# Two feed-forward networks of a four-layer transformer whose up products all read the un-normalised residual, and a norm spread over one of them

## The chip, the cores and the metric

The kernel runs on one core of a Trainium2 chip. The metric is the device time of one execution in microseconds (us). The engines are TensorE (PE: matmuls, with PEld for its weight loads), VectorE (DVE), ScalarE (ACT), GpSimd (POOL) and SyncE (SP), which here issues the DMAs of the weights.

## The reference

Two blocks of two layers each work on 256 context tokens and 256 latent tokens of 1024 features. A layer is a mixer (attention with pooling and gating in layers 0 and 1, mLSTM in layer 2, sliding-window attention in layer 3) and then a feed-forward network (FFN) with a squared relu. Each reads a root-mean-square norm of the residual with a scale and a shift per feature that come from a conditioning vector:

```python
h = h + g1 * mix
h = h + g2 * sq_relu_mlp(modulate(rms_norm(h, norm2_g[l]), sh2, sc2), w_ff1[l], w_ff2[l])
# rms_norm(x, g): x * rsqrt(mean(x*x) + eps) * g;  modulate(h, shift, scale): h * (1 + scale) + shift
# sq_relu_mlp(h, w1, w2): square(relu(h @ w1)) @ w2;  w1 is 1024 x 4096, w2 4096 x 1024
...
return rms_norm(h, final_g)          # end of the first block, layers 0 and 1
```

The second block starts from the first one's latent output and from a context of its own, ctx_2. Layers 1 and 3 are the last of their blocks: their FFNs work on the latent tokens alone.

## The kernel before

Features lie on the 128 partitions in KT = 8 chunks, tokens on the free axis, so the residual `h` is 128 x 8 x 512, context first (L = 256). A product is made in fp32r pairs: `whi·xhi`, `whi·xlo` and `wlo·xhi`, three matmuls, called a triple here. A weight tile of 512 KB (128 x 1024) comes by DMA into a staging tile (`raw` or `Y`), ScalarE copies it to `whi` (L116), and VectorE, or GpSimd where `self.wlow` says so, subtracts to get `wlo` (L130). Three buffers each hold `whi` and `wlo`; results go round the PSUM banks `mm`, `mm`, `mx`.

An FFN (`mlp`) has 32 up tiles and 32 down tiles, in eight groups q of four: `up(0)`, then `up(q)` and `down(q - 1)` in turn, and `down(7)` last. After an up tile ScalarE applies the relu, VectorE squares (L643), ScalarE makes the high part and VectorE the low part (L648) of the hidden tile. After a down tile VectorE adds to `h` (`add_to_h`, shown as h<-mm or h<-mx).

A norm begins in `add_to_h`: `square` lets ScalarE square a chunk of `h` that was just written, and GpSimd add it to `sums` (L509) for chunks 1 to 6, while the last square stays alone. `variance` lets TensorE multiply both with the constant `mean` (rows T<-mean), VectorE add eps (L521) and GpSimd take the power -0.5 (L522). `rows` spreads the result over the partitions (T<-ident). `modulate` then makes the high and low part of the normed chunk k with two VectorE instructions and one of ScalarE.

The generators given as `pre` and `mid` are advanced after so many steps of a group of three interleaved tiles, the numbers in `PRE` and `MID`; `PLAIN` is for the plain start. This start is what layers 1 and 3 have: their first three up tiles don't wait for the norm. They multiply the scaled residual (`plain_xs`, in the `Y` tiles), plus two columns with the shift, hence 258 columns; `evac_plain` then multiplies the result with the factor R (L659) and hands the extra column to the relu as its bias. From tile 4 on the FFN reads the normed `xs`. While this goes on GpSimd makes the low parts of the weights.

The first block's closing norm and layer 2's norm of the latent half are done together (`norm_twice`), with two squares for each chunk: one plain, one with the gain `fin`. Layer 2's norm of its own context (`own_context`) is written just before `down(7)` of layer 1's FFN.

A list scheduler orders each engine's instructions by priorities, so the order in the code is only the starting point.

## Time and profile before

| | |
|---|---|
| median of 3 runs | 2288.17 us (2285.65 to 2294.4) |
| profiled execution | 2289.41 us |
| its span, first to last instruction | 2287.6 us |
| mean granted TensorE clock | 0.983 |

The span is 1.8 us shorter than the execution's time. Rows below come from this one execution; their times count from the first instruction. Layer 1's FFN runs from about 1080 to 1285 us, layer 3's from about 2085 to the end. "Busy" is the time in which an engine has an instruction under way; "<-DVE h" after a wait names the engine and the tile that ended it.

### The profile page before, as it was taken

The page shows a single profiled execution, that of the slowest core. Times are in us where ns is not written, and L with a number is a line of the kernel's source. Part 1 is how long each engine was busy: PE and PEld are TensorE (multiplying, and loading weights), DVE is VectorE, ACT ScalarE, POOL GpSimd, SP SyncE. Part 2 cuts the span into 40 slices and gives each one's busy share as a digit, 9 for nine tenths or more (in the row PEclk, how much of TensorE's full clock was granted, in tenths as well). Part 3 has the DMA queues.
Part 4 walks back from the last instruction along what each step waited for, and adds up shares of the span by engine and source line. Part 5 has one row for each costly group of instructions (what it writes and reads, how often), then busy time and mean ns, then how long its engine had stood idle before and what let it go on. Part 6 is the DMA issues. An engine that isn't in the chain of part 4 may idle for free.

```text
span 2287.6 us, 36316 instructions
## 1 busy us (share of the span) xinstructions
PE 2184.0 (95%) x13402; PEld 1851.8 (81%) x13402; DVE 1623.2 (71%) x2762; ACT 1147.6 (50%) x2122; POOL 703.2 (31%) x566
## 2 busy tenths in 40 slices
PE   6999999999999999998999899999999999898998
PEld 3777777887777787898899877778777778878998
DVE  4877656687666875778877766778876566698766
ACT  3556434454443455655545646655443433675453
POOL 2640435424221543045300524253432222423001
PEclk9999999999999999999999999999999999999999
DMA  7451445446555443367554323344555532214552
GB/s 276 133 159 59 156 130 180 138 130 187 187 188 167 146 147 107 122 206 219 184 185 158 105 80 102 115 155 130 166 190 179 170 120 74 74 47 147 190 186 96
DMA packets 128146, 336.79 MB, mean 147 GB/s; under 512 B 14944, under 2 KB 24160, under 8 KB 127968
## 3 DMA queue, kind: packets, MB, share of 16 engines
q1 hardware_dynamic: 127968, 334.46, 45.1%
q8 instruction: 106, 1.74, 0.3%
q14 instruction: 72, 0.59, 0.1%
HBM read 333.36 MB, written 1.05 MB: 146 GB/s over the span
## 4 chain that ended last, share of the span: by engine, by line
PE 44%; DVE 7%; issue 3%; ACT 2%; POOL 1%; DMA 1%; DVEq 0%; POOLq 0%; ACTq 0%; SPq 0%
PE mm L122 27%; PE mx L122 11%; PE S L122 2%; DVE wlo L130 1%; PE pv L122 1%; PE T L122 1%; PE T L126 1%; PE num L122 1%; DVE macc L119 1%; ACT whi L116 1%; DMA mraw<-wmod_in 1%; DVE A L119 1%; POOL macc L449 1%; DVE T L119 0%; POOL sums L509 0%
## 5 line engine op out<-in xcount | busy, mean ns | idle before, releaser
L122 PE MATMUL mm<-A,whi 128*128 128x256 f32 (+1 forms) x2600 | 664.6, 343 | 17.7 <-ACT A L116 7.7
L449 POOL TENSOR_TENSOR macc<-macc,mraw 128x512 f32<-128x512 f32 x244 | 364.3, 1493 | 668.9 <-ACT mraw L116 659.9
L122 PEld LDWEIGHTS mm<-A,whi 128*128 128x128 f32 x2600 | 447.4, 191 | 86.2 <-issue 15.2
L122 PE MATMUL mm<-B,whi 128*128 128x256 f32 (+1 forms) x1884 | 457.8, 333 | 6.9 <-DVE B L119 3.8
L122 PE MATMUL mm<-A,wlo 128*128 128x256 f32 (+1 forms) x1300 | 442.0, 340 | 2.6 <-DVE wlo L130 2.6
L130 DVE TENSOR_TENSOR wlo<-raw,whi 128x1024 fp32r<-128x1024 f32 x252 | 345.3, 1372 | 135.3 <-ACT whi L116 133.9
L116 ACT ACTIVATE whi<-raw 128x1024 fp32r<-128x1024 f32 x273 | 287.6, 1056 | 274.5 <-PE mm L122 167.2
L122 PEld LDWEIGHTS mm<-B,whi 128*128 128x128 f32 x1884 | 320.7, 191 | 47.3 <-DVE B L119 4.3
L116 ACT ACTIVATE mraw<-mraw,silu 128x512 f32<-128x512 f32 x244 | 175.3, 722 | 294.5 <-DVE macc L119 180.2
L122 PE MATMUL mx<-A,whi 128*128 128x512 f32 (+1 forms) x1256 | 320.0, 342 | 1.6 <-ACT G L116 1.1
L122 PE MATMUL mm<-B,wlo 128*128 128x256 f32 (+1 forms) x942 | 312.0, 332 | 2.9 <-DVE wlo L130 1.6
L119 DVE SCALAR_TENSOR_TENSOR macc<-mraw,silu,macc 128x512 f32<-128x512 f32 x244 | 258.8, 1061 | 54.9 <-DMA mraw<-wmod_in 52.5
L122 PEld LDWEIGHTS mm<-A,wlo 128*128 128x128 f32 x1300 | 248.6, 191 | 30.3 <-DVE wlo L130 3.0
L116 ACT ACTIVATE whi<-Y 128x1024 fp32r<-128x1024 f32 x152 | 160.7, 1057 | 218.3 <-PE mm L122 154.1
L130 DVE TENSOR_TENSOR wlo<-Y,whi 128x1024 fp32r<-128x1024 f32 x148 | 192.2, 1298 | 90.7 <-ACT whi L116 90.6
L122 PEld LDWEIGHTS mx<-A,whi 128*128 128x128 f32 x1256 | 216.0, 190 | 31.1 <-issue 1.3
L122 PE MATMUL mx<-A,wlo 128*128 128x512 f32 (+1 forms) x628 | 214.9, 342 | 0.3 <-DVE wlo L130 0.3
L122 PE MATMUL mx<-B,whi 128*128 128x256 f32 (+1 forms) x836 | 201.2, 329 | 6.0 <-ACT B L116 3.1
L122 PEld LDWEIGHTS mm<-B,wlo 128*128 128x128 f32 x942 | 179.8, 191 | 21.6 <-DVE wlo L130 1.8
L509 POOL TENSOR_TENSOR sums<-sums,T 128x256 f32<-128x256 f32 x84 | 91.2, 1095 | 298.7 <-ACT T L116 297.2
L119 DVE SCALAR_TENSOR_TENSOR h<-mm,mod,h 128x256 f32<-128x256 f32 x278 | 125.8, 478 | 70.6 <-PE mm L122 70.4
L122 PEld LDWEIGHTS mx<-B,whi 128*128 128x128 f32 x836 | 141.1, 191 | 23.0 <-ACT B L116 3.8
(316 smaller groups left out, 3071.3 us busy)
## 6 DMA issues: line engine op xcount, KB each, us to landing
mraw<-wmod_in SPq DMA_DIRECT2D x352, 256.0 KB, 2.9
Y<-ff_in SPq DMA_DIRECT2D x152, 512.0 KB, 3.7
raw<-ff_in SPq DMA_DIRECT2D x104, 512.0 KB, 3.5
raw<-win_in SPq DMA_DIRECT2D x68, 512.0 KB, 3.8
raw<-mwin_in SPq DMA_DIRECT2D x17, 512.0 KB, 3.5
raw<-wo_in SPq DMA_DIRECT2D x16, 512.0 KB, 4.1
raw<-swin_in SPq DMA_DIRECT2D x10, 512.0 KB, 3.5
B<-wfirst_in SPq DMA_DIRECT2D x16, 256.0 KB, 5.4
```

Of the source, the lines that this page charges most:

```text
L116: return self.nc.scalar.activation(out, in_, func, **kw)
L119: return self.nc.vector.scalar_tensor_tensor(out, a, scalar, b, op0, op1)
L122: return self.nc.tensor.matmul(out, lhsT=lhsT, rhs=rhs, start=start, stop=stop, **kw)
L126: return self.nc.tensor.transpose(out, in_, self.ident[:k, :k])
L130: (eng or self.nc.vector).tensor_sub(lo, src, hi.bitcast(F32))
L449: self.nc.gpsimd.tensor_add(a1, a1, raw)
L509: (adder or self.nc.gpsimd).tensor_add(sums, sums, sq)
```

## The change

In layers 1 and 3 all 32 up tiles are plain: `mlp` gets `rows`, a list that holds the factor R, and every group of up tiles is evacuated by `evac_plain`. There is no normed `xs` there and no `modulate`; `factors` keeps R in a tile G. The plain `xs` lies in the A or B tiles instead of Y, so that the staging uses `raw, Y, Y` from the beginning, and `wlow` stays with VectorE.

Layer 2's context norm is `own_norm`, a generator that `mlp` advances once after each up group q = 1 to 7 of layer 1's FFN. `square` leaves the sum of chunks 6 and 7 to VectorE (the add into `pair`, L525 of the changed kernel); with a gain both squares of a chunk lie in one 512-wide Q tile and GpSimd adds them in one instruction. `PRE`, `MID` and `PLAIN` have other numbers.

```diff
-PRE, MID = (3, 6), (4, 11)
-PLAIN = (1, 2)
+PRE, MID = (4, 7), (6, 12)
+PLAIN = (3, 6)
...
-    def square(self, k, c0, c1, slot=None, adder=None, **kw):
-
-        slot = c0 // L if slot is None else slot
-        sums = self.sums[:, slot * L:(slot + 1) * L]
-        sq = sums if k == 0 else self.T1()
-        self.act(sq, self.h[:, k, c0:c1], AF.Square, **kw)
-        if 0 < k < KT - 1:
+    def square(self, k, c0, c1, adder=None, gain=None):
+
+
+        hv = self.h[:, k, c0:c1]
+        if gain is not None:
+            cols = slice(0, T)
+            sq = self.sums if k == 0 else self.t("Q")
+            self.act(sq[:, L:], hv, AF.Square)
+            self.act(sq[:, :L], hv, AF.Square, scale=gain[:, k:k + 1])
+        else:
+            cols = slice(c0, c1)
+            sq = self.sums[:, cols] if k == 0 else self.T1()
+            self.act(sq, hv, AF.Square)
+        slots = (CTX, LAT) if gain is not None else (c0 // L,)
+        sums = self.sums[:, cols]
+        if 0 < k < KT - 2:
             (adder or self.nc.gpsimd).tensor_add(sums, sums, sq)
+        elif k == KT - 2:
+            for s in slots:
+                self.sq_last[s] = sq[:, (s - slots[0]) * L:(s - slots[0] + 1) * L]
+            self.sq_pair = sq
         elif k:
-            self.sq_last[slot] = sq
+            pair = self.sq_pair if gain is not None else self.sq_last[slots[0]]
+            self.nc.vector.tensor_add(pair, pair, sq)
...
-    def plain_xs(self, A, S):
+    def plain_xs(self, tag, A, S):
 
 
 
 
         xs = []
-        for m in range(4):
-            y = self.t("Y", (P, 2, 2, L + 2), F32R)
-            xs += [(y[:, j, 0], y[:, j, 1]) for j in range(2)]
-            hi, lo = (y[:, :, i, L:] for i in range(2))
-            self.split(S[:, 2 * m:2 * m + 2], hi, lo)
+        for k in range(KT):
+            hi, lo = (self.t(tag, (P, L + 2), F32R) for _ in range(2))
+            xs.append((hi, lo))
+            self.split(S[:, k], hi[:, L:], lo[:, L:])
...
+    def factors(self, keep):
+
+        v = self.variance(LAT)
+        yield
+        keep.append(self.t("G", (P, L)))
+        self.act(keep[0], self.rows(v))
+
+    def norm(self, xs, s, A, S):
 
         v = self.variance(s)
         yield
         R = self.rows(v)
-        if s == CTX or keep is not None:
+        if s == CTX:
             pr, R = R, self.T1()
             self.act(R, pr)
-        if keep is not None:
-            keep.append(R)
         self.modulate(xs, s, A, S, R, range(KT))
+
+    def own_norm(self, src, A_S):
+
+
+
+        self.nc.sync.dma_start(self.h[:, :, :L], src)
+        for k in range(KT):
+            self.square(k, 0, L)
+        yield
+        r = self.variance(CTX)
+        A, S = A_S()
+        yield
+        pr = self.rows(r)
+        R = self.t("G", (P, L))
+        self.act(R, pr)
+        ts = [self.t("W", (P, 2, L)) for _ in range(3)] + [self.t("E", (P, 2, L))]
+        yield
+        for k in range(KT):
+            self.stt(ts[k // 2][:, k % 2], self.h[:, k, :L], A[:, k, CTX:CTX + 1], R,
+                     ALU.mult, ALU.mult)
+            if k % 4 == 3:
+                yield
+        xs = self.new_xs("A")
+        for k in range(KT):
+            t, (xh, xl) = ts[k // 2][:, k % 2], xs[k]
+            self.act(xh[:, :L], t, AF.Identity, bias=S[:, k, CTX:CTX + 1])
+            self.stt(xl[:, :L], t, S[:, k, CTX:CTX + 1], xh[:, :L].bitcast(F32),
+                     ALU.add, ALU.subtract)
+        yield xs, A, S
...
+            def evac_plain(j, ps, a, b):
+                c, t = self.sm(1), self.T1()
+                self.act(c, ps[:, L + LAT:L + LAT + 1])
+                self.nc.vector.tensor_mul(t, ps[:, :L], rows[0])
+                evac(j, t, L, T, c)
+
             aps = [w1[4 * q + j] for j in range(4)]
-            n = 0
-            if q == 0 and plain:
-                n = 3
-                rs, R = plain
-
-                def evac_plain(j, ps, a, b):
-                    c, t = self.sm(1), self.T1()
-                    self.act(c, ps[:, L + LAT:L + LAT + 1])
-                    self.nc.vector.tensor_mul(t, ps[:, :L], R[0])
-                    evac(j, t, L, T, c)
-
-                steps = Steps(kw.pop("pre"), PLAIN)
-                self.group([(j, self.wload(aps[j], KT)) for j in range(n)], lambda d: range(KT), rs,
-                           [(0, L + 2)], evac_plain, steps)
-                self.wlow = self.nc.gpsimd
-                kw = {}
-            self.gemm(aps[n:], xs, c0, lambda j, *r: evac(n + j, *r), **kw)
+            if rows is None:
+                self.gemm(aps, xs, c0, evac, **kw)
+            else:
+                js = list(range(4))
+                while js:
+                    m, steps = (3, Steps(kw.pop("pre"), PLAIN)) if kw else (1, None)
+                    kw = {}
+                    self.group([(j, self.wload(aps[j], KT)) for j in js[:m]], lambda d: range(KT),
+                               xs, [(0, L + 2)], evac_plain, steps)
+                    js = js[m:]
+                self.flush()
...
-        if not plain:
-            self.raws = cycle(["raw", "Y", "Y"])
+        self.raws = cycle(["raw", "Y", "Y"])
         up(0, head=3, pre=pre)
-        self.raws = cycle(["raw", "Y", "Y"])
         for q in range(1, 8):
             up(q)
             self.wlow = self.nc.vector
+            if other:
+                next(other, None)
             down(q - 1)
-        if before_last:
-            before_last()
...
-        rs, scale = b.plain_xs(A, S)
+        xs, scale = b.plain_xs("A", A, S)
         R = []
         b.gemm(aps, ys, c0, b.add_to_h(g1, then=scale), tail=3)
-        b.mlp(l, xs, c0, "B", pre=b.norm(xs, LAT, A, S, R), plain=(rs, R), **after)
+        b.mlp(l, xs, c0, "B", pre=b.factors(R), rows=R, **after)
...
             def own_context():
-                nc.sync.dma_start(b.h[:, :, :L], io["ctx2T"])
-                for k in range(KT):
-                    b.square(k, 0, L)
-                A, S = b.scales(2, 0)
-                xs2.extend(b.new_xs("A"))
-                b.whole(b.norm(xs2, CTX, A, S))
-                nc.vector.tensor_mul(A[:, :, LAT], A[:, :, LAT], b.fin[:, :KT])
-                xs2.append((A, S))
-
-            block1(b, ph, 1, st["xs"], pre(), dict(before_last=own_context, gain=b.fin))
-        A, S = xs2.pop()
+                yield
+                for xs in b.own_norm(io["ctx2T"], lambda: b.scales(2, 0)):
+                    if xs:
+                        xs2.extend(xs)
+                    yield
+
+            block1(b, ph, 1, st["xs"], pre(), dict(other=own_context(), gain=b.fin))
+        xs2, A, S = xs2
+        nc.vector.tensor_mul(A[:, :, LAT], A[:, :, LAT], b.fin[:, :KT])
```

The first place is TensorE at the start of layer 1's FFN. The 258-wide matmuls are the plain tiles, T<-mean are the products for the norm, and T with a number there is the last square alone. Before:

```order
L122 MATMUL mm_10293<-Y_9956,whi_10277 128x258 x2
L122 MATMUL mm_10293<-Y_9956,wlo_10278 128x258
L122 MATMUL T_10299<-mean,sums 128x1
L122 MATMUL mm_10293<-Y_9956,whi_10277 128x258 x2
L122 MATMUL mm_10293<-Y_9956,wlo_10278 128x258
L122 MATMUL mm_10293<-Y_9959,whi_10277 128x258 x2
L122 MATMUL mm_10293<-Y_9959,wlo_10278 128x258
L122 MATMUL mm_10294<-Y_9956,whi_10283 128x258 x2
L122 MATMUL mm_10294<-Y_9956,wlo_10284 128x258
L122 MATMUL T_10299<-mean,T_2031_10271 128x1
L122 MATMUL T_10299<-mean,sums 128x1
L122 MATMUL T_10299<-mean,T_2031_10271 128x1
```

After (T_2025 is the sum of the last two squares):

```order
L122 MATMUL mm_10298<-A_9940,whi_10287 128x258
L122 MATMUL mm_10298<-A_9941,whi_10287 128x258
L122 MATMUL mm_10298<-A_9940,wlo_10288 128x258
L122 MATMUL T_10312<-mean,sums 128x1
L122 MATMUL mm_10297<-A_9952,whi_10281 128x258
L122 MATMUL mm_10297<-A_9953,whi_10281 128x258
L122 MATMUL mm_10297<-A_9952,wlo_10282 128x258
L122 MATMUL mm_10298<-A_9944,whi_10287 128x258
L122 MATMUL mm_10298<-A_9945,whi_10287 128x258
L122 MATMUL mm_10298<-A_9944,wlo_10288 128x258
L122 MATMUL mm_10297<-A_9956,whi_10281 128x258
L122 MATMUL mm_10297<-A_9957,whi_10281 128x258
```

Four triples, the fourth's rows among those shown, stand ahead of the first T<-mean instead of one, and the second T<-mean, which needs the last square, is 3.3 triples further on instead of three.

The second place is VectorE at the same point, from the last chunk of the residual (h<-mx) on. T<-h,A,T and A<-T,mod,A are `modulate`; L659 is the product with R. Before, the end of that stretch:

```order
L119 SCALAR_TENSOR_TENSOR T_2054_10336<-h,A_1_9938,T_2048_10314 128x256
L119 SCALAR_TENSOR_TENSOR T_2055_10340<-h,A_1_9938,T_2048_10314 128x256
L119 SCALAR_TENSOR_TENSOR A_9947<-T_2052_10328,mod_96,A_9946 128x256
L119 SCALAR_TENSOR_TENSOR T_2056_10344<-h,A_1_9938,T_2048_10314 128x256
L119 SCALAR_TENSOR_TENSOR A_9949<-T_2053_10332,mod_96,A_9948 128x256
L659 TENSOR_TENSOR T_2058_10415<-mm_10293,T_2048_10314 128x256
L119 SCALAR_TENSOR_TENSOR A_9951<-T_2054_10336,mod_96,A_9950 128x256
L643 TENSOR_TENSOR Q_10420<-Q_10418 128x256
L119 SCALAR_TENSOR_TENSOR A_9953<-T_2055_10340,mod_96,A_9952 128x256
L648 TENSOR_TENSOR B_10423<-Q_10420,B_10422 128x256
L119 SCALAR_TENSOR_TENSOR A_9955<-T_2056_10344,mod_96,A_9954 128x256
L659 TENSOR_TENSOR T_2064_10427<-mm_10294,T_2048_10314 128x256
```

After, from the last chunk to the first evacuations (L525 is the new add, L698 the product with R, now by the G tile, L130 the low parts of weights):

```order
L119 SCALAR_TENSOR_TENSOR h<-mx_10248,g_1_9936,h 128x256
L130 TENSOR_TENSOR wlo_10294<-Y_10291,whi_10293 128x1024
L525 TENSOR_TENSOR T_2025_10244<-T_2025_10244,T_2027_10274 128x256
L119 SCALAR_TENSOR_TENSOR A_9969<-h,A_1_9938,A_9968 128x256
L535 TENSOR_SCALAR sm_10317<-T_10312 128x2
L130 TENSOR_TENSOR wlo_10425<-raw_10422,whi_10424 128x1024
L698 TENSOR_TENSOR T_2046_10387<-mm_10297,G_10345 128x256
L130 TENSOR_TENSOR wlo_10468<-Y_10465,whi_10467 128x1024
L688 TENSOR_TENSOR Q_10392<-Q_10390 128x256
L698 TENSOR_TENSOR T_2052_10399<-mm_10298,G_10345 128x256
L693 TENSOR_TENSOR B_10395<-Q_10392,B_10394 128x256
L698 TENSOR_TENSOR T_2058_10411<-mx_10299,G_10345 128x256
```

The modulate rows are gone; the product with R of the first tile (T_2046) stands behind the weight split of tile 4 (wlo_10425) and ahead of that of tile 5.

The third place is GpSimd from the middle of layer 1's FFN to layer 2, in the changed kernel. The 256-wide sums are those of layer 2's context, the 512-wide ones those of the residual with and without gain:

```order
L536 TENSOR_TENSOR sm_10318<-sm_10317,m_88 128x2
L518 TENSOR_TENSOR sums<-sums,T_2173_10947 128x256
L518 TENSOR_TENSOR sums<-sums,T_2174_10950 128x256
L518 TENSOR_TENSOR sums<-sums,T_2175_10953 128x256
L518 TENSOR_TENSOR sums<-sums,T_2176_10956 128x256
L518 TENSOR_TENSOR sums<-sums,T_2177_10959 128x256
L536 TENSOR_TENSOR sm_11281<-sm_11280,m_88 128x2
L518 TENSOR_TENSOR sums<-sums,Q_12739 128x512
L518 TENSOR_TENSOR sums<-sums,Q_12775 128x512
L518 TENSOR_TENSOR sums<-sums,Q_12793 128x512
L518 TENSOR_TENSOR sums<-sums,Q_12811 128x512
L518 TENSOR_TENSOR sums<-sums,Q_12829 128x512
```

Before, twelve 256-wide additions of this kind (`sums<-sums,T`, L509) stand in the place of the five 512-wide ones, and the context's own stand at the start of the FFN.

## Rows read from the trace of the kernel before

**Rows 1.** The page, its first part: busy us (share of the span) xinstructions.

```profile
PE 2184.0 (95%) x13402; PEld 1851.8 (81%) x13402; DVE 1623.2 (71%) x2762; ACT 1147.6 (50%) x2122; POOL 703.2 (31%) x566
```

**Rows 2.** By stage: length; busy of PE, PEld, DVE, ACT, POOL; clock, DMA share, GB/s.

```profile
1060.00:1120.00 60.00, 50.83 (x372) 49.43 (x370) 52.41 (x63) 33.95 (x67) 34.82 (x23) 0.89 0.59 187
1120.00:1255.00 135.00, 135.00 (x1138) 135.00 (x1139) 96.21 (x143) 66.37 (x95) 0.00 (x0) 1.00 0.54 176
1255.00:1312.00 57.00, 49.72 (x371) 47.62 (x370) 44.30 (x71) 33.24 (x67) 29.16 (x27) 0.91 0.31 101
```

**Rows 3.** TensorE's timeline, layer 1's FFN start: start, length, instruction [idle before].

```profile
1079.94 0.58 PE L122 MATMUL T<-mean,sums 128*128 128x1 f32 x2 [2.59 <-POOL sums L509]
...
1087.18 0.40 PE L122 MATMUL mm<-Y,whi 128*128 128x258 f32 x2
...
1092.23 0.41 PE L122 MATMUL mx<-Y,whi 128*128 128x258 f32 x2
...
1097.36 0.76 PE L122 MATMUL mm<-A,whi 128*128 128x256 f32 x2 [4.26 <-DVE T L659]
```

**Rows 4.** The chain that ended last, inside the FFN: start, length, what.

```profile
1132.99 5.69 PE mm L122 x48
```

**Rows 5.** Four stretches of low clock (columns as in rows 2).

```profile
1079.57:1086.40 6.83, 6.46 (x30) 6.46 (x31) 2.69 (x5) 1.22 (x3) 1.03 (x2) 0.50 0.61 186
1096.64:1103.47 6.83, 6.11 (x29) 6.14 (x29) 5.55 (x10) 3.85 (x9) 2.38 (x1) 0.50 0.28 106
1281.00:1284.40 3.40, 3.40 (x18) 3.40 (x17) 3.40 (x4) 1.53 (x4) 3.40 (x4) 0.50 0.64 205
2103.57:2107.00 3.43, 3.43 (x16) 3.27 (x16) 2.65 (x8) 1.32 (x3) 0.00 (x0) 0.50 0.83 290
```

**Rows 6.** VectorE's timeline at layer 1's FFN start.

```profile
1080.10 0.47 DVE L119 SCALAR_TENSOR_TENSOR h<-mx,g,h 128x256 f32<-128x256 f32 x1
...
1093.93 2.56 DVE L119 SCALAR_TENSOR_TENSOR T<-h,A,T 128x256 f32<-128x256 f32 x1
...
1096.80 0.41 DVE L659 TENSOR_TENSOR T<-mm,T 128x256 f32<-128x256 f32 x1
```

**Rows 7.** GpSimd's timeline at the same place.

```profile
1090.97 5.24 POOL L130 TENSOR_TENSOR wlo<-raw,whi 128x1024 fp32r<-128x1024 f32 x2 [6.24 <-ACT whi L116]
```

**Rows 8.** Groups by line inside the FFN, 1120 to 1255, VectorE and ScalarE.

```profile
L130 DVE TENSOR_TENSOR wlo<-Y,whi 128x1024 fp32r<-128x1024 f32 x32 | 39.2, 1226 | 21.5 <-ACT whi L116 21.4
...
L643 DVE TENSOR_TENSOR Q<-Q 128x256 f32<-128x256 f32 x24 | 10.0, 419 | 0.0
...
L116 ACT ACTIVATE whi<-Y 128x1024 fp32r<-128x1024 f32 x31 | 32.9, 1060 | 45.3 <-PE mm L122 33.2 <-PE mx L122 12.1
```

**Rows 9.** TensorE's waits, 1255 to 1312: total, times, longest.

```profile
PE T L122 <- POOL sums L509: 2.5, 1, 2.5
PE mm L122 <- DVE wlo L130: 1.6, 1, 1.6
PE T L122 <- POOL sm L522: 1.1, 1, 1.1
```

**Rows 10.** GpSimd's groups by line, 1255 to 1312: busy, mean ns, idle before.

```profile
L509 POOL TENSOR_TENSOR sums<-sums,T 128x256 f32<-128x256 f32 x12 | 13.6, 1169 | 9.0 <-ACT T L116 9.0
```

**Rows 11.** TensorE's waits, 2075 to 2120.

```profile
PE mm L122 <- DVE B L119: 3.4, 1, 3.4
PE mm L122 <- POOL wlo L130: 1.3, 1, 1.3
PE T L122 <- POOL sums L509: 1.2, 1, 1.2
```

**Rows 12.** TensorE's waits, 820 to 870, 1540 to 1580, 1930 to 1950.

```profile
PE T L122 <- POOL sums L509: 1.4, 1, 1.4
...
PE T L122 <- POOL sums L509: 1.9, 1, 1.9
...
PE T L122 <- POOL sums L509: 1.7, 1, 1.7
```

More of the change, by code (lines that the diff above doesn't have):

```diff
@@ L577, in plain_xs @@
         return xs, scale
-    def norm(self, xs, s, A, S, keep=None):
+    def factors(self, keep):
[4 more added lines that the diff above has]
+    def norm(self, xs, s, A, S):
         v = self.variance(s)
@@ L618, in evac @@
                     if squares:
-                        self.square(d, a, b)
-                        if gain is not None:
-                            self.square(d, a, b, CTX, scale=gain[:, d:d + 1])
+                        self.square(d, a, b, gain=gain)
                     if then:
@@ L624, in add_to_h, with mlp @@
         return evac
-    def mlp(self, i, xs, c0, tag, pre=None, mid=None, before_last=None, gain=None, plain=None):
+    def mlp(self, i, xs, c0, tag, pre=None, mid=None, other=None, gain=None, rows=None):
         w1, w2 = self.io[f"ff1_{i}"], self.io[f"ff2_{i}"]
@@ L994, in block1 @@
     aps = [io[f"wo{l}"][d] for d in range(8)]
-    xs = b.new_xs("A")
     if l == 0:
+        xs = b.new_xs("A")
         b.gemm(aps, ys, c0, b.add_to_h(g1), tail=3, mid=b.norm(xs, LAT, A, S))
@@ L1328, in block2_swa @@
     A, S = b.scales(i, 1)
-    rs, scale = b.plain_xs(A, S)
+    xs, scale = b.plain_xs("B", A, S)
     b.gemm2([io["swout"][1, d] for d in range(4)], at[4:], L,
             b.add_to_h(b.mod[i][:, 2], then=scale), tail=1)
-    xs, R = b.new_xs("B"), []
-    b.mlp(i, xs, L, "A", pre=b.norm(xs, LAT, A, S, R), plain=(rs, R))
+    R = []
+    b.mlp(i, xs, L, "A", pre=b.factors(R), rows=R)
 def build(tc, io):
```

## The prediction

> **What bounds the kernel now.** I read the busy shares first, then tables by stage, then, in the stages that are not full, TensorE's waits and its timeline. TensorE is busy 95% of the span, VectorE 71%, ScalarE 50%, GpSimd 31% [rows 1]: only time in which TensorE stands still, or runs at the lower clock, can be won. The stage table says where that is. Inside layer 1's FFN TensorE is busy 135.00 of 135 us at a granted clock of 1.00; at its start it is busy 50.83 of 60 at 0.89, at its end 49.72 of 57 at 0.91 [rows 2]. Layer 3's FFN has the same two faces, but its end belongs to the output. So the gain is at seams and the interior is only at risk.
>
> Two prices are needed throughout. At the full clock a triple of 258-wide matmuls (whi·hi, whi·lo, wlo·hi) goes by in 0.361 us (14 triples from 1087.18 to 1092.23 [rows 3]), a 256-wide matmul in 118.5 ns (5.69 us for 48 [rows 4]), so a matmul of 258 columns costs 1.7 ns more. And a stretch at clock 0.50, that is 1.2 instead of 2.4 GHz, costs half of its length: 3.4 us for the two long ones of 6.83 us, 1.7 us for the short ones of about 3.4 us [rows 5]. The two long ones begin within 1 us of the ends of the two standstills in rows 3.
>
> **Part 1, start of layer 1's FFN.** In the trace TensorE stands 2.59 us before the mean matmul (1079.94) and 4.26 us before tile 4, which begins at 1097.36 because its input, or the bank that VectorE must empty for it, is late [rows 3]. The empty-out (L659, 0.41 us) starts only at 1096.80, since it is queued in VectorE's order behind modulate instructions, two of which took over 2.5 us instead of 0.47 [rows 6] while GpSimd made the low parts of two weight tiles, 5.24 us [rows 7]. The change removes all 16 modulate instructions and GpSimd's weight tiles from this place, so what is late next is one chain: h of chunk 7, square, the new VectorE add, mean, then the weights of tile 4.
>
> h(7) starts at 1080.10 now. Its predecessors on VectorE are the same, less some waiting, so I put it at 1079.6; the weight split ahead of the add takes 1.23 [rows 8], the add as much as the nearest two-input instruction of that size, 0.42 [rows 8], so the sum is there at about 1081.6 and the mean matmuls end at about 1082.4. TensorE has four triples ahead of the first mean matmul instead of one, and 3.3 more ahead of the second; 16.7 of the 24 remain: 16.7 x 0.361 = 6.0, with the rows of R 6.3, so the group ends near 1088.7. Tile 4's weights need tile 0's buffers, which come free 8 triples (2.9 us) before the end; copy 1.06, split 1.23, empty-out 0.41 [rows 6, 8] make 2.7 behind one another, plus hand-overs: I allow 0.5 of wait. Tile 4 begins at 1089.2 instead of 1097.36: **8.1 us**. The half-clock stretch after the removed wait (from 1097.36 on 6.1 us of it) gives back 3.05; I charge one short stretch, 1.7, for the waits that stay. Net **-9.4**. Bounds: if the first half-clock stretch lasts to 1086.40 as now, 4.0 us at twice the pitch cost 1.8 more, and with no stretch given back it is -6.3; with every wait gone -12.5.
>
> **Part 2, end of layer 1's FFN and start of layer 2.** TensorE waits 2.5 for GpSimd's sums, 1.6 for a weight split of VectorE and 1.1 for GpSimd's power [rows 9]. The sums are late because 12 additions run back to back, 13.6 us [rows 10]. The context norm's 16 modulate instructions and its variance are here too. After the change the norm's steps lie between the eight groups of the FFN, so 1.6 and 1.1 go. GpSimd has five 512-wide adds; none of that shape reads PSUM or is in another place of my rows, so they are bounded by the 256-wide one (1.17) below and two of these (2.34) above: 5.8 to 11.7 us instead of 13.6, begun no later, and the last chunk's two squares no longer pass through it. In place of the 2.5 stands a VectorE add of 512 columns behind two ScalarE squares, twice 0.42 by rows 8, of which I leave 0.8 as a wait. 5.2 - 0.8 = 4.4. Three short stretches at 0.50 lie in this place, one of them in rows 5; I take two and a half back, 4.25. Net **-8.7**, between -4.4 (two waits and one stretch) and -11.
>
> **Part 3, start of layer 3's FFN.** Waits of 3.4 for modulate's result, 1.3 for a GpSimd split, 1.2 for the sums [rows 11]. The first two have no counterpart in the new kernel; of the third I take 0.7; the new wait for tile 4's weights is 0.5 as in part 1: 4.9. The stretch at 0.50 behind the 3.4 us [rows 5] gives 1.7. Net **-6.6**, between -4.9 and -8.6 (if the sums and weights are never waited for).
>
> **Part 4, the other norms.** Three more seams wait for GpSimd's sums, 1.4, 1.9 and 1.7 us [rows 12]. They now add one product less on GpSimd, and one on VectorE (0.42 [rows 8]); the later waiting point (PRE and MID) has one more triple or two ahead of it. At the ends of the FFNs of layers 0 and 2 I take 2.0 each, about 1.2 of wait and half a short stretch; at layer 2's output projection nothing, because the add is queued on VectorE behind a sum of modulation weights. Other small seams and the tail, where VectorE is needed for the last squares, come to -0.2. Net **-4.2**, between 0 and -9.
>
> **Part 5, what it costs inside the FFNs.** 29 newly plain tiles in each of two FFNs, 24 matmuls each, 1.7 ns: **+2.4**. Each of these tiles gets a VectorE multiplication, 0.41 [rows 6], and a one-column copy on ScalarE, which is no longer than the 1.06 of a whole weight tile [rows 8]. A tile of weights is used for 24 x 118.5 ns = 2.84 us. VectorE is busy 96.21 of 135 and ScalarE 66.37 [rows 2]; The 29 multiplications add 11.9, and the context norm 16 instructions of 0.47 and one add, 8: 116 of 135. That is 86%, so the mean leaves room, and the cover is 19 us. I take +0.3, and 0 to 8 as bounds, the upper one if all of the norm's work fell on TensorE.
>
> GpSimd's rows have no instruction inside this stretch now: 0.00 busy [rows 2]. The change puts five additions there. What such company does is seen in rows 6 and 7: 0.47 became 2.56 under a GpSimd instruction. So up to 5 x 1.17 = 5.8 us of VectorE may be blocked, once; against the 19 us of room that is hidden. The Trainium skill, SBUF — State Buffer, section Who interferes with whom, says that a VectorE instruction with two SBUF inputs and a GpSimd instruction that reads SBUF exclude one another; the trace agrees at 1093.93, and by it alone the adds would cost VectorE at most what they last.
>
> The 1 MB of context moves on SP's queue in either kernel while the FFN's weights stream at 176 GB/s, DMA share 0.54 [rows 2]: about 6 us of transfer with nothing behind it that is needed at once. Taken at nothing; if it holds up a weight tile, it costs up to 3.
>
> **Sum.** -9.4 - 8.7 - 6.6 - 4.2 + 2.4 + 0.3 = -26.2. The profiled execution took 2289.41, so 2263.2; it lies 1.2 above the median of the three runs (2288.17), so against that **2262.0**. A measurement of this kernel tells about 0.5% (11.4 us) from no change.
>
> **Rivals.**
> *The stretches at half clock stay* (0.22). They follow standstills, and some will remain at each seam. Then nothing is given back by them and each part stands near its smaller bound: -6.3 - 4.4 - 4.9 - 1 + 2.4 = -14.2, **2274**. For it: even the 2.59 us wait carries 6.83 us at 0.50 behind it. Against: the longest two waits, 4.26 and 3.4, go entirely.
> *The context norm was never what held layer 2 up* (0.08). If its seam waits for the squares of the latent half, whose sums are as late, part 2 is -4.4 while the rest holds: **2266**. For it: the longest wait there is for sums.
> *VectorE becomes the bound inside the plain FFNs* (0.04), the one on the other side. Its place is every eviction: TensorE's bank waits for the empty-out, which is queued behind two weight splits of 1.23, and now needs 0.41 and then the ScalarE relu before the bank's successor. With 29 + 29 tiles it needs 26 / 58 = 0.45 us of new standstill per tile to eat the whole gain; from there to the case that all of the 0.41 and of ScalarE's bound of 1.06 are exposed (85 us) it gives **2288 to 2347**. Against it: 135.00 of 135 and 29% of VectorE idle in the same stage, where the empty-out of a bank has two other banks' time, 5.7 us, to be done.
> *The moves do not arrive* (0.03): the scheduler keeps the weights of tile 4 late behind the factor's chain (mean, power, rows, copy), and the gap of 4.26 comes back as one of 3 at the same place: part 1 about -3, part 3 about -3: **2272**.
>
> **Numbers.** The forecast's own case has 0.63, range 2249 to 2268. Eight in ten, with the first rival's 2274 and the lower bounds of the sum (-39 in all): 2249 to 2275. Faster by over 0.5%, that is below 2276.7: 0.92, from the first case and nearly all of the first, second and fourth rivals; within: 0.05, from the first rival's upper end and the third's lower; slower: 0.03.
>
> **What would show it.** Right: no TensorE wait over 1 us between the third and fourth up tile of layers 1 and 3's FFNs; tile 4 about 8 us sooner after h(7); clock of the two start stages above 0.93; no wait for sums over 1 us at the seam into layer 2; the interior still full. Wrong: TensorE below 133 of 135 in the interior, waits there for VectorE's empty-out or split, or a new wait on the factor copy G or the new add.

## The result, and the profile after

The changed kernel took 2264.12 us (median of 4 runs, 2260.49 to 2268.6) against 2291.28 for the kernel before: ratio 0.9882, 95% interval 0.9864 to 0.9901. Forecast was 2262.0. Measured again beside later experiments it had 0.9901 (0.9884 to 0.9919). The profiled execution has a span of 2262.5 us at a mean clock of 0.990, before 2287.6 at 0.983.

First the page's busy shares, answering to [rows 1]:

```profile
PE 2173.8 (96%) x13402; PEld 1842.8 (81%) x13402; DVE 1617.1 (71%) x2819; ACT 1150.1 (51%) x2172; POOL 657.0 (29%) x537
```

Then the stages that answer to [rows 2] (length; busy PE, PEld, DVE, ACT, POOL; clock, DMA share, GB/s), with the start of layer 3's FFN last:

```profile
1060.00:1120.00 60.00, 56.55 (x460) 55.36 (x460) 49.10 (x71) 34.38 (x62) 15.20 (x11) 1.00 0.60 189
1120.00:1250.00 130.00, 129.62 (x1077) 129.42 (x1076) 102.89 (x173) 70.20 (x128) 4.72 (x6) 1.00 0.52 169
1250.00:1290.00 40.00, 39.45 (x327) 38.74 (x326) 29.64 (x48) 26.75 (x53) 15.66 (x18) 1.00 0.31 98
2045.00:2095.00 50.00, 48.40 (x406) 46.96 (x405) 38.89 (x69) 31.51 (x64) 6.13 (x6) 1.00 0.45 148
```

The three seams at which the change aims run at clock 1.00 now, where [rows 2, 5] have 0.89, 0.91 and stretches of 0.50. Standing at 1 - 0.983 of the span's clock before and 1 - 0.990 now, the slower clock cost about 39 us and costs 23: up to 16 of the 25 us between the two spans are clock. The rest, and what the wider matmuls cost, is waiting.

TensorE's timeline and VectorE's at the start of layer 1's FFN, answering to [rows 3, 6], ScalarE's copy for tile 4 not shown:

```profile
1080.17 0.28 PE L122 MATMUL T<-mean,sums 128*128 128x1 f32 x2
...
1082.21 0.38 PE L122 MATMUL T<-mean,T 128*128 128x1 f32 x2 [0.43 <-DVE T L525]
...
1089.07 0.40 PE L122 MATMUL mx<-A,whi 128*128 128x258 f32 x2
...
1089.43 0.46 PE L122 MATMUL mm<-A,whi 128*128 128x258 f32 x2
```

```profile
1080.21 0.47 DVE L119 SCALAR_TENSOR_TENSOR h<-mx,g,h 128x256 f32<-128x256 f32 x1
1080.61 1.21 DVE L130 TENSOR_TENSOR wlo<-Y,whi 128x1024 fp32r<-128x1024 f32 x1
1081.74 0.41 DVE L525 TENSOR_TENSOR T<-T,T 128x256 f32<-128x256 f32 x1
...
1087.77 1.23 DVE L130 TENSOR_TENSOR wlo<-raw,whi 128x1024 fp32r<-128x1024 f32 x1 [4.54 <-ACT whi L116]
1088.92 0.42 DVE L698 TENSOR_TENSOR T<-mm,G 128x256 f32<-128x256 f32 x1
```

h(7) stands where it stood, 1080.2; the mean matmul on the sums waits for nothing, the one on the new add 0.43 us, and tile 4 follows the group without a gap at 1089.43 instead of 1097.36. The split and the empty-out that it needs end 0.4 and 0.1 us before it, so this is just in time.

TensorE's waits, layer 1's FFN start, then the seam into layer 2 (1240 to 1300), then layer 3's FFN start (2045 to 2110): total, times, longest.

```profile
PE mx L122 <- DVE wlo L130: 1.7, 1, 1.7
PE mm L122 <- DVE wlo L130: 1.1, 2, 0.6
PE T L122 <- DVE T L525: 0.4, 1, 0.4
...
PE T L122 <- POOL sums L518: 0.4, 1, 0.4
...
PE mm L122 <- DVE h L119: 1.0, 1, 1.0
PE mx L122 <- DVE h L119: 0.5, 1, 0.5
```

Of the waits in [rows 9] the 2.5 has become 0.4 and the other two are gone; of those in [rows 11] all three are gone.

To place all of it I take from each trace, for every matmul, the step to the next one's start less the step that its width has at the full clock (118.7 ns at 256 columns, 120.2 at 258, 120.4 at 260). The sum over a stage is what TensorE lost there to waits and to the lower clock. Stages are cut at the same place of the program in each kernel (in and out: the starts and ends of the FFNs). One profile each; a stage that an edit leaves alone can differ by 4 us from one profile to the next (layer 1 has 24.6 for e1 and 28.7 for the changed kernel's second profile, and e1's edit lies behind that stage). The column heads are explained with the experiments; "again" is the changed kernel a second time.

```
us lost       before   changed     again  e4 plain  e9 squares  e1 norm at end  e2 old squares       e10       e11
FFN 0 out       10.3       6.0       6.0      10.3         6.0             7.6             8.7       6.0       7.6
layer 1         26.0      28.1      28.7      26.2        28.0            24.6            28.2      28.5      25.4
FFN 1 in        17.1       5.9       5.7       8.3        15.2             5.7             8.1       7.0       5.5
FFN 1           -0.0       2.4       2.5       1.1        -0.0             1.1             1.9       1.5       0.4
FFN 1 out       16.3       2.7       2.7      17.8        13.0            13.5             7.6       2.7      13.5
layer 2         34.4      34.6      36.8      32.9        29.8            29.8            35.8      35.8      29.9
FFN 2 in         8.4      11.2      11.1       8.4         9.0             9.6             6.2       7.8       6.2
FFN 2 out        6.8       6.0       7.5       6.8         6.8             6.0             7.7       8.6       7.5
FFN 3 in        11.5       3.0       2.7       7.4        10.7             2.7             4.4       2.8       2.9
FFN 3           -0.0       1.1       0.9       0.9        -0.0             0.9             0.9       0.4       0.3
```

The gain is at the seams: 11.2 and 8.5 us at the two plain starts, 13.6 at the seam into layer 2, 4.3 at the end of layer 0's FFN. It is paid for with 2.8 at the start of layer 2's FFN and with about 3.5 in the two interiors. Of these 3.5, 2.6 are the wider matmuls, which mostly step by 122.1 ns and not by the 120.2 taken out here (1.9 ns x 24 x 58 tiles); the step from 118.7 to 120.2 is 2.1 us more, which the table leaves out.

### The profile page after: what moved, and what is told of

It is laid out like the page before. It is cut to its first block, busy times and chain, and to the rows that moved or that the text cites. A ratio compares the mean times of both kernels' runs of the same rounds, so it can differ in the third digit from the quotient of the medians.

```text
span 2262.5 us, 36381 instructions
## 1 busy us (share of the span) xinstructions
PE 2173.8 (96%) x13402; PEld 1842.8 (81%) x13402; DVE 1617.1 (71%) x2819; ACT 1150.1 (51%) x2172; POOL 657.0 (29%) x537
## 4 chain that ended last, share of the span: by engine, by line
PE 45%; DVE 6%; ACT 3%; issue 3%; DMA 2%; POOL 1%; DVEq 0%; POOLq 0%; ACTq 0%; SPq 0%
PE mm L122 27%; PE mx L122 11%; PE S L122 2%; PE pv L122 1%; DVE wlo L130 1%; PE T L122 1%; PE T L126 1%; PE num L122 1%; DMA mraw<-wmod_in 1%; ACT whi L116 1%; DVE macc L119 1%; DVE A L119 1%; DVE B L119 1%; DVE T L119 1%; POOL macc L449 1%
## 5 line engine op out<-in xcount | busy, mean ns | idle before, releaser
L122 PE MATMUL mm<-A,whi 128*128 128x512 f32 (+2 forms) x2632 | 672.0, 342 | 12.1 <-ACT A L116 7.3
L122 PE MATMUL mm<-B,whi 128*128 128x512 f32 (+2 forms) x1916 | 461.9, 331 | 4.5 <-DVE B L130 1.3
L122 PE MATMUL mm<-A,wlo 128*128 128x512 f32 (+2 forms) x1316 | 445.6, 339 | 3.7 <-DVE wlo L130 3.7
L130 DVE TENSOR_TENSOR wlo<-raw,whi 128x1024 fp32r<-128x1024 f32 x250 | 340.0, 1362 | 130.4 <-ACT whi L116 125.8
L116 ACT ACTIVATE whi<-raw 128x1024 fp32r<-128x1024 f32 x265 | 279.0, 1055 | 250.8 <-PE mm L122 144.4
L122 PE MATMUL mx<-A,whi 128*128 128x512 f32 (+2 forms) x1272 | 323.1, 341 | 1.6 <-ACT G L116 1.1
L122 PE MATMUL mm<-B,wlo 128*128 128x512 f32 (+2 forms) x958 | 315.6, 330 | 0.9 <-DVE wlo L130 0.9
L130 DVE TENSOR_TENSOR wlo<-Y,whi 128x1024 fp32r<-128x1024 f32 x160 | 209.1, 1307 | 86.3 <-ACT whi L116 85.4
L122 PE MATMUL mx<-A,wlo 128*128 128x512 f32 (+2 forms) x636 | 216.2, 340 | 0.7 <-DVE wlo L130 0.7
L122 PE MATMUL mx<-B,whi 128*128 128x256 f32 (+2 forms) x852 | 204.4, 327 | 8.0 <-ACT B L116 3.3
L518 POOL TENSOR_TENSOR sums<-sums,T 128x256 f32<-128x256 f32 x60 | 64.1, 1074 | 340.3 <-ACT T L116 339.1
## 6 DMA issues: line engine op xcount, KB each, us to landing
mraw<-wmod_in SPq DMA_DIRECT2D x352, 256.0 KB, 2.9
B<-wfirst_in SPq DMA_DIRECT2D x16, 256.0 KB, 5.4
```

The source lines that it names most:

```text
L116: return self.nc.scalar.activation(out, in_, func, **kw)
L122: return self.nc.tensor.matmul(out, lhsT=lhsT, rhs=rhs, start=start, stop=stop, **kw)
L130: (eng or self.nc.vector).tensor_sub(lo, src, hi.bitcast(F32))
L518: (adder or self.nc.gpsimd).tensor_add(sums, sums, sq)
```

## The experiments

**One part alone, or one part undone.** The question was which part carries the 27 us.

e4 has only the plain FFNs: it is the changed kernel with the edits of e1, e2 and e8 below taken together, of which this is the context norm's:

```diff
-                for xs in b.own_norm(io["ctx2T"], lambda: b.scales(2, 0)):
...
+                xs2.append(b.new_xs("A"))
+                b.whole(b.norm(xs2[0], CTX, A, S))
```

> Only the plain FFNs: squares, context norm and the three pairs of numbers as before. Theory: the starts of the two FFNs give 11 and 8.5 less the 2 to 3 us of waits for sums, the wider matmuls and the interior cost 4 to 5: 12 to 15 below before, ratio 0.994. Rival: without the other two parts the waits for sums at the starts eat most of it: less than 8 below before, ratio above 0.9965.

Measured: 2286.3, ratio 0.9982 (0.9968 to 0.9996), some 4 us below before: the rival's side. Locally the theory holds, -8.8 and -4.1 at the two starts, but the waits for sums stand where they stood. TensorE's waits at layer 1's start (1061 to 1117) in this kernel:

```profile
PE T L122 <- POOL sums L509: 2.6, 1, 2.6
PE mx L122 <- DVE wlo L130: 1.7, 1, 1.7
```

e9 is the kernel before with the new `square` alone:

```diff
-                        self.square(d, a, b)
-                        if gain is not None:
-                            self.square(d, a, b, CTX, scale=gain[:, d:d + 1])
+                        self.square(d, a, b, gain=gain)
```

> The kernel before with one part of the change, the new squares (chunks 1 to 5 added on GpSimd, chunks 6 and 7 on VectorE, 512-wide with a gain); FFNs, context norm and the three pairs of numbers are as before. The changed kernel with the old squares took 13 us more than the changed kernel. Theory: that is an interaction, the squares pay only where the other parts have cleared VectorE for the new add, so alone they give 3 to 6 us, ratio 0.998. Rival: they give their 13 us by themselves, ratio 0.9943.

Measured: 2277.91, ratio 0.9937 (0.9919 to 0.9954). The rival is right: the squares pay by themselves, about 14 us. TensorE's waits for sums over the whole span of the kernel before,

```profile
PE T L122 <- POOL sums L509: 12.3, 8, 2.6
```

are 1.3 us in e9, and three waits for the new add, 5.4 in all, have come in their place. It is not an interaction: e2, the changed kernel with only the old `square`, loses as much.

```diff
+        if 0 < k < KT - 1:
+            (adder or self.nc.gpsimd).tensor_add(sums, sums, sq)
+        elif k:
+            self.sq_last[slot] = sq
```

> The changed kernel, with the squares as before: chunks 1 to 6 added on GpSimd, 256 wide, the last square a matmul part of its own. Theory: the waits for GpSimd's sums come back, 2.5 us at the seam into layer 2 with one stretch at half clock, 1 to 2 us at three other seams: 5 to 9 us above the changed kernel, ratio about 0.992. Rival: with the later waiting points and without the context norm's additions nearby, GpSimd is in time anyway: within 2 us of the changed kernel.

Measured: 2277.31, ratio 0.9938 (0.9923 to 0.9953), 13 us above the changed kernel, more than the 5 to 9 of the theory. The waits for sums that come back, as TensorE's waits over its whole span show them, 8.4 us in 7 places:

```profile
PE T L122 <- POOL sums L509: 8.4, 7, 2.1
```

In the stages 2.7 are at FFN 0 out, 4.9 at FFN 1 out, 2.2 and 1.4 at the plain starts; at FFN 2 in, though, the old squares lose 5.0 less.

e8 has the changed kernel with the old PRE, MID and PLAIN.

```diff
-PRE, MID = (4, 7), (6, 12)
-PLAIN = (3, 6)
+PRE, MID = (3, 6), (4, 11)
+PLAIN = (1, 2)
```

> The changed kernel with PRE, MID and PLAIN as before, so that the norm's matmuls stand earlier in TensorE's order. Theory: the sums are in time only because the waiting points moved too: waits of 1 to 2 us with a half-clock stretch return at two or three seams, 4 to 8 us above the changed kernel, ratio about 0.991. Rival: with one product less on GpSimd the old points are late enough: within 2 us of the changed kernel.

Measured: 2267.22, ratio 0.9890 (0.9867 to 0.9912): the rival in time. A part of the waits does return, 2.4 us for sums in four places instead of 0.6 in two, and FFN 1 out loses 4.8 instead of 2.7; the time doesn't show it.

**The spread context norm.** e1 makes it whole again before down(7):

```diff
-            if other:
-                next(other, None)
             down(q - 1)
+        if other:
+            other()
```

> The changed kernel, with layer 2's context norm whole again just before down(7) of layer 1's FFN. Theory: the context norm's modulate and variance held up the seam into layer 2 (the waits of 1.1 and 1.6 us and the stretches at half clock behind them), so TensorE loses 8 to 11 us between 1247 and 1294 instead of 3.4, and the time is 5 to 8 us above the changed kernel, ratio to before about 0.991. Rival: that seam's gain came from the squares (five 512-wide additions and the VectorE add), then the time is within 2 us of the changed kernel and the loss at the seam stays under 5.

Measured: 2271.13, ratio 0.9904 (0.9889 to 0.9919). At the seam the theory is right and too low: it loses 13.5 instead of 2.7, with waits (1244 to 1299) that the changed kernel lacks:

```profile
PE mm L122 <- DVE h L119: 2.1, 2, 1.2
PE mm L122 <- DVE A L119: 1.3, 3, 0.8
PE mm L122 <- DVE wlo L130: 1.2, 2, 0.8
PE T L122 <- POOL sm L536: 1.1, 1, 1.1
```

But of 10.8 us at the seam only 5 are left in the time by the first ratio of the changed kernel (0.9882), and less than 1 by the second (0.9901). Layer 2 loses 29.8 with the norm at the end and 34.6 and 36.8 with it spread. In the changed kernel ScalarE empties a bank (Q<-mm) late, behind its work for layer 2's gates and a weight copy, and TensorE waits for it where e1 waits for nothing:

```profile
1304.52 0.57 ACT L116 ACTIVATE Q<-mm 128x512 f32<-128x512 f32 x1
```

```profile
1305.15 0.50 PE L122 MATMUL mm<-whi,A 128*128 128x512 f32 x1 [1.74 <-ACT Q L116]
```

The spread norm is not the only way to this wait: the kernel before, with its norm at the end and the old squares, has it too, 2.8 us. Only the kernels with the new squares and the norm at the end (e1, e9, e11) lack it, and they are the three that lose 29.8 to 29.9 in layer 2.

e11, below, repeats the comparison with another pair.

**Was it modulate, or GpSimd beside it?** e3 is the kernel before with VectorE making the low parts at the plain start:

```diff
-                self.wlow = self.nc.gpsimd
```

> The kernel before, with the low parts of the weights at the plain start made by VectorE instead of GpSimd. Theory: modulate itself is what delays tile 4; VectorE loses the blocked 2 to 4 us but gains two to three splits of 1.2, so the waits of 4.3 and 3.4 shrink by 1 to 2 us each and the time falls by 3 to 6, ratio 0.998. Rival: the company of GpSimd was the trouble, then both waits go below 1 us, their half-clock stretches too, and the time falls by 12 to 15, ratio 0.994.

Measured: 2286.24, ratio 0.9971 (0.9958 to 0.9984), between the two. The long waits are gone without any plain tile more: in layer 1 tile 4 waits 0.62 us, and not for the product with R, where [rows 3] have 4.26; in layer 3 it waits 0.56 for its weights where [rows 11] have 1.3, and not at all for modulate's result, where they have 3.4.

```profile
1098.34 0.39 PE L122 MATMUL mm<-A,wlo 128*128 128x256 f32 x1 [0.62 <-DVE wlo L130]
...
2094.11 0.39 PE L122 MATMUL mm<-B,wlo 128*128 128x256 f32 x1 [0.56 <-DVE wlo L130]
```

So the rival names the cause of the long waits. Yet FFN 3 in falls only from 11.5 to 7.2 and FFN 1 in from 17.1 to 16.2: in layer 1 the 2.6 for sums stays, waits of 1.7 and 0.7 for h and 1.4 for a hidden tile come up behind it, and the plain tiles remove more than those long waits.

**The width.** e5, and e6 with (0, L + 4) and the shift copied twice, are the changed kernel with

```diff
-                               xs, [(0, L + 2)], evac_plain, steps)
+                               xs, [(0, L)], evac_plain, steps)
```

> The changed kernel with plain tiles 256 columns wide: the two columns with the shift are left out of the products, and the relu's bias is read from column 0 instead, so the shift of these two FFNs is missing from the result. In the changed kernel the mean step from one 258-wide matmul to the next is 122.1 ns from tile 4 on, where 120.3 was measured for the interleaved first three tiles. Theory: the width alone costs this, the step falls to 118.7 to 119 and TensorE's time in the two FFNs by 4.5 to 5 us; the time by 4 to 5, ratio 0.986. Rival: the step stays near 121 to 122, since it is the evacuation of the plain tiles that costs it: time unchanged within 1 us.

> The changed kernel with plain tiles 260 columns wide, the two columns with the shift standing there twice. Theory: the step grows with the width, 1.6 ns for a column as from 256 to 258: about 125 ns, 4.5 to 5 us more in the two FFNs. Rival: 258 is an awkward width and 260 goes at 120.5 or below: 2 us or more are saved.

Measured: 2260.67, ratio 0.9856 (0.9831 to 0.9882), and 2265.49, 0.9879 (0.9858 to 0.9900). The chain that ended last, inside layer 1's FFN, 48 matmuls of the plain tiles in the changed kernel, in e5 and in e6:

```profile
1145.38 5.87 PE mm L122 x48
```

```profile
1167.62 5.69 PE mm L122 x48
```

```profile
1170.26 5.76 PE mm L122 x48
```

That is 122.3, 118.5 and 120.0 ns. e5's theory holds: the width alone costs it, about 4.5 us in the two FFNs (3.4 ns x 24 x 58 tiles = 4.7). In e6 the rival holds: 260 columns go by faster than 258. The 1.5 ns of these two stages (means of 120.6 against 122.1) are the most that the traces have: elsewhere it is 120.9 to 121.1 against 121.5 to 122.2, about 1 ns, which is 1 to 2 us in all and too little for the times to show.

**The cover of the evacuation.** e7 makes the product with R twice in all 64 plain tiles:

```diff
+                t2 = self.T1()
+                self.nc.vector.tensor_mul(t2, t, rows[0])
-                evac(j, t, L, T, c)
+                evac(j, t2, L, T, c)
```

> The changed kernel with the product with R made twice, one more VectorE instruction of 0.42 us in the chain of each of the 64 plain tiles, so that the result holds the factor twice. Theory: the evacuation is hidden, TensorE loses at most 2 us more in both FFNs, and the time stays within 3 us of the changed kernel. Rival (VectorE as the bound): 0.2 to 0.42 us for each tile, 13 to 27 us more.

Measured: 2273.51, ratio 0.9920 (0.9905 to 0.9935); the changed kernel, measured beside it, had 2266.0 and 0.9901. Neither end: 7.5 us by the medians, 4 by the ratios, whose intervals overlap. Layer 1's FFN, 1120 to 1240, in that kernel, and a wait from it:

```profile
1120.00:1240.00 120.00, 116.72 (x965) 115.02 (x963) 105.15 (x176) 65.59 (x115) 16.19 (x13) 1.00 0.58 188
```

```profile
PE mx L122 <- DVE T L698: 1.5, 1, 1.5
```

By the traces, 4.7 and 2.5 us more are lost in the two FFNs and 4.8 at FFN 1 out. In layer 1's FFN VectorE is at 88% and TensorE waits for it, but not for the products alone: the scheduler has put seven sums of modulation weights here too, on VectorE and on GpSimd (16.19 us busy, 4.72 in the changed kernel). In layer 3's FFN, where GpSimd does nothing, 2.5 are lost with VectorE at 79% (110.94 of 140), the share at which layer 1's FFN hid the first product. So a second product is not wholly hidden, and the busy share alone does not tell when.

**A version from these.** In FFN 2 in, the new add is late. VectorE's, GpSimd's and TensorE's timelines of the changed kernel:

```profile
1524.54 1.39 DVE L119 SCALAR_TENSOR_TENSOR macc<-mraw,silu,macc 128x512 f32<-128x512 f32 x1 [1.85 <-DMA mraw<-wmod_in]
1525.85 0.47 DVE L119 SCALAR_TENSOR_TENSOR h<-mm,mod,h 128x256 f32<-128x256 f32 x1
1527.14 1.28 DVE L525 TENSOR_TENSOR T<-T,T 128x256 f32<-128x256 f32 x1 [0.82 <-ACT T L116]
```

```profile
1526.87 1.27 POOL L449 TENSOR_TENSOR macc<-macc,mraw 128x512 f32<-128x512 f32 x1 [1.49 <-ACT mraw L116]
```

```profile
1528.48 0.44 PE L122 MATMUL T<-mean,T 128*128 128x1 f32 x2 [3.01 <-DVE T L525]
```

VectorE waits for a DMA ahead of h(7), and the add, 0.41 at the start of layer 1's FFN, takes 1.28 beside a GpSimd addition. The Trainium skill, SBUF — State Buffer, section Who interferes with whom, has a VectorE instruction with two SBUF inputs and a GpSimd instruction that reads SBUF exclude one another; the two times agree with it, since the add ends 0.28 us after the GpSimd addition (1528.42 and 1528.14). e10 uses the old sums at this one place, and 260 columns; e11 is e10 with the context norm at the end again.

```diff
+        if 0 < k < KT - 2 + (not self.pairs):
...
+        elif k and not self.pairs:
+            self.sq_last[slots[0]] = sq
...
+    b.pairs = False
     b.gemm([io["mwout"][d] for d in range(8)], ys, 0, b.add_to_h(b.mod[i][:, 2]), tail=3,
```

> The changed kernel once more, beside the next two on the same chip: ratio to before 0.988, and the stages of its profile within 2 us of the first one's, above all 34 us of loss in layer 2 and 11 us at the start of layer 2's FFN, where three other kernels had 30 and 9.

> The changed kernel with the old sums (chunk 6 on GpSimd, the last square by itself) at layer 2's output projection alone, and plain tiles 260 columns wide. Theory: the add there is late behind the modulation sums and costs 3 to 5 us at the start of layer 2's FFN (11.2 us lost, 6.2 with the old squares), and 260 columns save 1.5 ns for each of 1392 matmuls, 2 us: 5 to 7 us below the changed kernel, ratio to before 0.985 to 0.986. Rival: the start of layer 2's FFN was late in that one profile by chance: only the 2 us.

> The kernel of the run before (old sums at layer 2's output projection, 260 columns; ratio 0.9874) with layer 2's context norm whole again just before down(7) of layer 1's FFN. At the seam into layer 2 the spread norm saved 10.8 us, but the three profiles of kernels with the new squares or 260 columns and a spread norm lost 35 to 37 us in layer 2, those with the norm at the end and new squares 29.8. Theory: half of the saving comes back there, so this kernel loses 13 us at the seam, 30 in layer 2, and takes 3 to 6 us more than the one before it, ratio 0.989 to 0.990. Rival: all of it comes back, ratio 0.987 to 0.988.

Measured: the changed kernel 2266.0, ratio 0.9901; e10 2262.77, 0.9874 (0.9860 to 0.9887); e11 2258.29, 0.9869 (0.9846 to 0.9891). FFN 2 in was no chance, 11.1 again, although e1, with the same code there, has 9.6; the wait for the add is 3.0 in all three. e10 brings the stage to 7.8, with this in place of the 3.01:

```profile
PE T L123 <- POOL sums L519: 1.1, 1, 1.1
```

e10 is 3 us below the changed kernel beside it by the medians and 6 by the ratios, whose intervals overlap, so whether the 5 to 7 expected are there stays open. Between e11 and e10 the rival holds: e11 loses 10.8 us more at the seam, but 5.9 less in layer 2, 1.1 less in FFN 1 and 1.6 less in FFN 2 in, and it is not slower. Some 2 us of the spread norm's saving are left by these stages; the times, each known to 3 to 5 us, can't tell that from nothing.

## Why the prediction was right, and where its terms were off

The total, 2262.0 against 2264.12, is right. Parts 1 and 3 went as told; part 2 named the waits at its seam, but not what their removal is worth; part 4 had one place with the wrong sign. The sizes were off in both directions, and that the total came so close is in part luck: by the traces the five parts come to -30.0 us instead of -26.2 (part 5 with all of the width), and stages that the prediction left out lose 4.9 more than before, which brings the span to -25.1. The second profile of the same kernel has -29.2 and 11.8.

Part 1. Forecast 1089.2 for tile 4, found 1089.43; the sum of the squares is there at 1082.15 and the mean matmuls end at 1082.59, 0.55 and 0.2 later than forecast, and in exchange the wait of 0.5 for tile 4's weights does not show. I charged one more short stretch at half clock; there is none. -11.2 instead of -9.4, of which e4 and e9 give 8.8 to the plain tiles and 1.9 to the squares.

Part 2 was sized -8.7 and its seam gave -13.6, beyond its bound of -11. The sum took the waits of [rows 9] alone; the kernel before has three smaller ones there (1.0, 0.4 and 0.2), which are gone too. The outer bounds of parts 2 and 3 do not come out of their rows: all waits and stretches named there make 10.3 and 7.6, not 11 and 8.6. All three stretches of half clock went, and the sums are waited for 0.4. GpSimd's five 512-wide additions lie inside the bounds, by the group of 1240 to 1300:

```profile
L518 POOL TENSOR_TENSOR sums<-sums,Q 128x512 f32<-128x512 f32 x5 | 8.1, 1624 | 109.2 <-ACT Q L116 109.0
```

What the sum lacked is the other side: it booked the seam's gain as gain of the kernel. From the first addition of down(6) in layer 1's FFN to the first one of layer 2's output projection, VectorE's additions to h, it takes 264.0 us before, 256.0 with the squares alone (e9), 250.6 and 252.8 with all, 254.9 with all but the spread norm (e1). So the squares give 8.0 of the seam and layer 2 together, and the norm that I thought was the larger part 2 to 4 (3.3 between e10 and e11, 251.8 and 255.1). In the time of e10 and e11 it can't be seen. The second rival (the norm was never what held layer 2 up) was wrong about the seam and nearly right about the time.

Part 3: -8.5 instead of -6.6; two waits for h, 1.0 and 0.5, are left, and no stretch at half clock.

Part 4: FFN 0 out -4.3 and FFN 2 out -0.8 against 2.0 each, FFN 2 in +2.8 against nothing. Its reason, the add queued behind a modulation sum, was the right place to look, and the DMA ahead of it makes it a loss. This is also the one sign of being wrong that came: TensorE waits for the new add, over the whole span of the changed kernel

```profile
PE T L122 <- DVE T L525: 4.8, 3, 3.0
```

The waits for sums, 12.3 us before and 0.6 now, fell by more.

Part 5 was too low for the width, +2.4 against about 4.5: the price came from one stretch of the kernel before (120.2 ns), and most of the new tiles step by 122.2. That tiles are interleaved or not does not decide this, as the last section shows. The rest of the interior was hidden but for 0.9 us, as forecast, at 79% VectorE rather than 86; the five GpSimd additions of the context took 3.9 us there in all, and TensorE waited 0.4 for an h. e7 shows how near the bound was.

e4's small gain adds up in its profile, with one point open. It gains 12.9 us at two starts and loses 2.0 in the interiors, 2.1 by the width that the table leaves out, 1.5 at FFN 1 out and 2.9 in its layer 3 ahead of the FFN; layer 2 gives 1.5 back. That makes 5.9, and its span is 4.8 shorter than before's. The 2.9 lie where this edit changes nothing, and one profile can't say whether they are the edit's or chance.

The rival that nothing is given back by the clock is refuted by the three 1.00 of the stage table; the one that VectorE becomes the bound is refuted for this kernel, and a next product brings it near (e7).

## What to carry to other kernels

Cut the sum of a norm's last additions short before rewriting what reads it: here one add moved from GpSimd's queue to VectorE, and two squares made one instruction, gave about 14 of 23 to 27 us, more than the two larger edits. A gain at a seam is not yet a gain of the kernel: measure up to the next point at which another engine's chain ends, since that chain takes up what TensorE saved. And a moved add costs what stands ahead of it on its new queue, a DMA's wait too.

## What the runs showed of the hardware

Steps from one matmul's start to the next one's, at full clock and without a wait: 118.7 ns for 256 columns. For 258 columns in the changed kernel there are two steps, which hold for whole tiles: 120.0 and 122.2. The expectation of e5 sets interleaved first tiles against later single ones, but that is not what parts the two steps. At layer 1's FFN the first profile of the changed kernel has the last of the interleaved tiles at 120.0 and the single ones at 122.2; the second profile of the same kernel has the interleaved ones at 122.2, the next five single ones at 120.0 and the others at 122.2. For 260 columns (e6) the two steps are 120.0 and 121.1. Means over the single tiles of an FFN are 121.5 to 122.2 for 258 columns (seven profiles) and 120.6 to 121.1 for 260 (three), so two columns more are about 1 ns cheaper. What puts a tile at one step or the other, no run here tells.
